# Output copies of the last heads at high priority, low halves of later weights behind the last 1/std of a layer, and another order of V, of the last norm and of the first logits

## The chip, the cores and the metric

One core of one Trainium2 chip runs the whole kernel as one program. The metric is the time on the device in microseconds (us). The kernel before takes 1009.29 us, the median of three runs (1008.67 to 1011.96).

A core has five engines, each with its own queue of instructions, which it works off in the order in which they were put there: TensorE (PE in the profile; PEld is its loading of weights), VectorE (DVE), ScalarE (ACT), GpSimd (POOL) and SyncE (SP), which here issues the DMAs. An instruction that needs another engine's result waits for a semaphore, and all that stands behind it on its engine waits with it.

## The reference

A decoder trunk of four layers over 512 tokens of width 1024, in float32. Layer i uses mixer i mod 3, so the layers (counted from 0) are latent attention (MLA), sliding-window attention (SWA), forgetting attention (FoX), MLA. Each branch has one input projection that also gives a gate; after each stands a LayerNorm over the residual:

```python
def reference(x, ln_g, ln_b, ...):
    for i in range(DEPTH):                     # DEPTH = 4
        ...
        x = _layernorm(DEEPNORM_ALPHA * x + y, ln_g[i], ln_b[i])

def _fox_branch(x, w_in, b_f, w_out):
    h = x @ w_in
    q, k, v = ...                              # 16 heads of 64
    f_logit = h[..., 3 * W:3 * W + FOX_HEADS]
    cum = jnp.cumsum(jax.nn.log_sigmoid(f_logit + b_f), axis=1)
    o = _dense_causal(q, k, v, FOX_HEAD_DIM ** -0.5, cum)
    return (o * jax.nn.silu(gate)) @ w_out
```

MLA projects x to 672 columns (384 for the query, 256 for key and value, 32 for the rotary key), norms them, and projects these up to heads; its causal attention is like FoX's without the gates.

## The kernel before, in words

**Arithmetic.** Every float32 operand is split in a high half, rounded to the type that TensorE takes (fp32r), and a low half, the rest. A product is three matmuls: high by high, high by low, low by high. For weights the high half is a cast on ScalarE (L306) and the low half a subtraction on GpSimd (L310), from a raw tile `wr` that SyncE loaded; for activations ScalarE casts the high half and VectorE subtracts (L325). A *unit* is one piece of weights of up to 1024 columns. `W(key)` (called where a projection begins) sees to it that the unit and up to three behind it are split; `hold` is the last unit that it may go ahead to; `_split(i)` splits all units up to i. A unit has an even and an odd tile in the tables below: `w` high, the next `w` low.

**A layer.** The normed x of 512 tokens is kept transposed, `xT` (high and low), in four token blocks of 128. First come projections from `xT`: for MLA the compressed columns in two groups T0 and T1 of 336 columns for each token block (`t_block`, order `T_ORDER`), 24 matmuls each, whose results VectorE copies to `cqk` and ScalarE squares for `t_norm`; for FoX the first V groups, V0 (256 columns and the 16 gate logits, 272) and V1 (256), 24 matmuls for each token block (`vproj`). Three PSUM banks (`pp`) take such results. Then 16 heads run interleaved with the remaining projections: logits (`ss`), softmax, transposes of the probabilities (`ptt`) and the product with V (`oo`), whose two halves are added by a copy on ScalarE and an addition on VectorE (L543, L544) into `o`; there is one bank for `oo`. The output projection (`po`, `pp`) ends the layer.

**What sets the order.** During the heads TensorE's order is written out by hand: the strings in `ORDER`, one for each layer, take steps of the logits (s), the transposes (t), the products with V (o) and the other projections (f, g, h); `TAIL` does it for the last two heads. In `finish` the string `FINISH[layer]` sets VectorE's order: for token block t, `r t` (or `h t`, `i t` for its halves) adds the output projection to the residual in tile `r` with its sum, `s t` starts the sum of squares on ScalarE, `t t` computes 1/std, whose power runs on GpSimd (L646, `stat<-stat,half`), `a t` scales by mean and gain, `b t` by 1/std with the bias (both L660, two instructions of 512 columns), and `x t` transposes the block into the next layer's `xT` (`pxt` L389, eight transposes, a cast on ScalarE, the low half on VectorE). All that no string sets (ScalarE, GpSimd, SyncE, and TensorE outside the heads) is ordered when the kernel is built, by a scheduler with costs of its own; `high_priority` makes it prefer what stands inside. Of the last layer the last block is normed in halves (`p`, `q`), the scaled result goes into tile `y`.

**The start.** Blocks of x are loaded and transposed; `mla(0)` begins with T0 and T1 while raw weights still arrive.

Of the kernel before, what the change touches and what calls it, by code (L numbers as in the profile page):

```python
# [16 lines left out]
ALU = mybir.AluOpType  # L17
# [12 lines left out]
QR, KR = 384, 256  # L30
# [13 lines left out]
)  # L44
PRO = ((2, 1, 2, 2), (2, 1, 19, 0))
TAIL = ((3, 4, 6, 6), (2, 10, 2, 5), (9, 0, 4, 9), (6, 3, 7, 2))


VF_COLS, VF_K = 256 + H, (3, 3, 2)
T_COLS = 336  # L50
T_ORDER = (((0, 0), (0, 1), (1, 0), (1, 1), (0, 2), (1, 2), (0, 3), (1, 3)),
           ((0, 0), (1, 0), (0, 1), (1, 1), (0, 2), (1, 2), (0, 3), (1, 3)))

def jobs(s):
# [12 lines left out]
ORDER = (  # L67
# [133 lines left out]
class Net:  # L201
# [178 lines left out]
    def x_transposes(self, xt, tb, banks=None):  # L380

        nc = self.nc
        for g in range(2):
            pool, tag = banks or (self.ps_t, "pt")
            ps = pool.tile([128, 512], F32, tag=tag, name=self.nm("pxt"))
            for k in range(4):
                c = (4 * g + k) * 128
                v = ps[:, k * 128:(k + 1) * 128]
                nc.tensor.transpose(v, xt[:, c:c + 128], self.ident[:])  # L389
# [3 lines left out]
            nc.scalar.copy(hi, src)  # L393
            self.lo(lo, src, hi)
# [130 lines left out]
    def attn_pv(self, h, st):  # L525
        nc = self.nc
# [11 lines left out]
        p, odd = divmod(h, 2)  # L538
# [3 lines left out]
        a, b = (slice(64, 128), slice(0, 64)) if odd else (slice(0, 64), slice(64, 128))  # L542
        nc.scalar.copy(o[a, :], o_ps[b, :])  # L543
        nc.vector.tensor_tensor(o[a, :], o_ps[a, :], o[a, :], op=ALU.add)  # L544
        if odd:
# [82 lines left out]
    def ln_other_half(self, st, tb):  # L628

        nc = self.nc  # L630
        e, s = st["half"], st["stat"][:, tb]
        nc.vector.tensor_scalar(s[:, 2:3], s[:, 0:1], s[:, 1:2], -1.0 / D, op0=ALU.add, op1=ALU.mult)
        jk = self.p_g.tile([128, D // 2], BF16, tag="g", name=self.nm("jk"))
        nc.scalar.activation(jk[:], st["r"][tb][:, D // 2:], AF.Square, bias=s[:, 2:3], scale=1.0, accum_out=e[:, 2:3])
        nc.vector.tensor_tensor(e[:, 3:4], s[:, 2:3], e[:, 0:1], op=ALU.subtract)
        nc.vector.tensor_scalar(e[:, 3:4], e[:, 3:4], e[:, 3:4], D / 2.0, op0=ALU.mult, op1=ALU.mult)
        nc.vector.tensor_tensor(e[:, 3:4], e[:, 3:4], e[:, 1:2], op=ALU.add)

    def ln_rstd(self, st, tb):
# [5 lines left out]
        nc.vector.tensor_scalar(s, s, 1.0 / D, LN_EPS, op0=ALU.mult, op1=ALU.add)
        nc.gpsimd.tensor_tensor(s, s, self.half[:, 0:1], op=ALU.pow)  # L646

    def ln_apply(self, layer, st, tb, part):
        nc = self.nc
# [3 lines left out]
        src = r  # L653
        if halves and part == 0:

            r = st["r"][tb] = self.p_wr.tile([128, D], F32, tag="wr", name=self.nm("y"))
        for c in range(2):
            cols = slice(c * 512, (c + 1) * 512)
# [60 lines left out]
    def finish(self, layer, st):  # L719
        nc = self.nc  # L720
        self.load_gb(layer, st)
        self.layer = layer + 1
        if layer < DEPTH - 1:
            self.new_xT()
# [13 lines left out]
        def ends(tb):  # L738
            assert st["done"] >= (84, 105, 126, 147)[tb]
            mm(0, tb)  # L740
            if tb < 3:
# [4 lines left out]
                "r": lambda t: (res(t, 0), res(t, 1)), "h": lambda t: res(t, 0), "i": lambda t: res(t, 1), "s": S0, "t": S1,  # L746
                "a": lambda t: A(t, 0), "b": lambda t: A(t, 1), "p": lambda t: self.ln_half(st, t), "q": lambda t: self.ln_other_half(st, t), "x": X}
        if "p3" in FINISH[layer]:
            st["halves"] = NT - 1
            st["half"] = self.p_st.tile([128, 4], F32, tag="half", name=self.nm("half"))  # L750
        with self.tc.manual_schedule(engines={mybir.EngineType.DVE}):
            for w in FINISH[layer].split():
                todo[w[0]](int(w[1:]))

    def cq_done(self, layer):
# [12 lines left out]
    def mla(self, layer):  # L768
# [19 lines left out]
        def t_norm(tb):  # L788
# [5 lines left out]
            with self.tc.high_priority():  # L794
                nc.gpsimd.tensor_tensor(rr[:, tb, :], rr[:, tb, :], self.half[:, :2], op=ALU.pow)
            nc.vector.tensor_scalar(x[:, :QR], x[:, :QR], rr[:, tb, 0:1], None, op0=ALU.mult)
            nc.vector.tensor_scalar(x[:, QR:QR + KR], x[:, QR:QR + KR], rr[:, tb, 1:2], None, op0=ALU.mult)
            kr, c, d = x[:, 640:672], x[:, 672:704], x[:, 704:736]
# [6 lines left out]
        self.hold = self.index[(layer, "T", 1, 3)]  # L805
        for t, tb in T_ORDER[layer > 0]:
            if (t, tb) == (1, NT - 1):
                self.hold = len(self.units)
            t_block(t, tb)
            if t == 1:  # L810
                t_norm(tb)
# [94 lines left out]
        vs = {}  # L906
# [135 lines left out]
    def fox(self, layer):  # L1042
# [9 lines left out]

        for tb in range(NT):
            self.run(self.vproj([(layer, "V", 0, b) for b in range(3)], 8, self.xblk, vs, 0, [tb], f_logit))
            self.run(vp(1, [tb]))
        nc.scalar.activation(e[:], z[:], AF.Abs)
# [52 lines left out]
def trunk(ctx, tc, t):  # L1109
# [13 lines left out]
    for tb in range(NT):  # L1123
        net.x_transposes(x0[tb], tb)
    for layer in range(DEPTH):
        (net.mla, net.swa, net.fox)[layer % 3](layer)
# [31 lines left out]
```

## Time and profile before

| | |
|---|---|
| profiled execution | 1012.59 us |
| its span | 1010.8 us |
| granted TensorE clock, mean | 0.993 |
| median of three runs | 1009.29 us |
| busy: TensorE, ScalarE, VectorE, GpSimd | 981.7, 620.0, 599.2, 505.4 us |

The busy time of an engine is the time in which it executes something; the idle times of TensorE and what ended them are in the views that the prediction quotes. A row of a timeline has its start, its length, the engine, the line of the kernel, the operation, and output and inputs by name; consecutive instructions of one group make one row with their number, and the brackets hold the idle time before it and what it waited for.

### The profile page before, as it was taken

What the parts mean: (1) busy time and instruction counts of PE and PEld (TensorE: products, weight loads), DVE (VectorE), ACT (ScalarE), POOL (GpSimd) and SP (SyncE); (2) the same over time, 40 slices, a digit from 0 to 9 for tenths busy, and PEclk for the clock granted to TensorE, in tenths of its full rate; (3) what the DMA queues carried; (4) which work ended last, traced back from release to release, by engine and by line L of the source; (5) the groups of instructions that cost most, each with busy time, mean ns of one, the idle gap of its engine ahead of it and who ended that gap; (6) DMA issues with size and microseconds to landing.
All of it is one profiled execution on the core that took longest, in us unless ns stands there. A gap on an engine that the chain in (4) does not pass through costs nothing.

```text
span 1010.8 us, 16221 instructions
## 1 busy us (share of the span) xinstructions
PE 981.7 (97%) x5512; PEld 854.6 (85%) x5512; DVE 599.2 (59%) x1509; ACT 620.0 (61%) x1355; POOL 505.4 (50%) x568
## 2 busy tenths in 40 slices
PE   8999999999999999999999999999999999999996
PEld 8978888878888888888988898888779888888785
DVE  2467676944736667729324655567456476668827
ACT  4378888753256777723446766666443588888722
POOL 5846656334146663433455757553263746664211
PEclk9999999999999999999999999999999999999999
DMA  6453332543542222334344334326233354324322
GB/s 224 124 151 87 112 87 85 165 154 98 188 125 84 75 73 101 112 99 150 102 140 125 105 85 146 104 82 186 88 117 114 108 137 129 94 87 123 107 63 84
DMA packets 37795, 116.79 MB, mean 116 GB/s; under 512 B 5440, under 2 KB 5696, under 8 KB 37456
## 3 DMA queue, kind: packets, MB, share of 16 engines
q1 hardware_dynamic: 37712, 115.75, 36.9%
q8 instruction: 44, 0.72, 0.3%
q14 instruction: 39, 0.32, 0.1%
HBM read 92.62 MB, written 8.42 MB: 100 GB/s over the span
## 4 chain that ended last, share of the span: by engine, by line
PE 45%; DVE 3%; issue 3%; POOL 2%; ACT 1%; DMA 1%; DVEq 0%; POOLq 0%; SPq 0%; ACTq 0%
PE pp L322 30%; PE ss L322 4%; PE po L322 4%; PE oo L322 3%; PE ptt L514 3%; POOL w L310 1%; DVE r L660 1%; PE pxt L389 1%; DMA cb<-cd 0%; DVE PT L325 0%; DMA q<-rq 0%; ACT PT L500 0%; DVE r L590 0%; DVE wo L310 0%; PE pc L823 0%
## 5 line engine op out<-in xcount | busy, mean ns | idle before, releaser
L322 PE MATMUL pp<-xT,w 128*128 128x512 f32 (+1 forms) x1440 | 352.5, 387 | 0.0
L310 POOL TENSOR_TENSOR w<-wr,w 128x512 fp32r<-128x512 f32 (+1 forms) x202 | 241.9, 1223 | 193.4 <-ACT w L306 128.2
L322 PEld LDWEIGHTS pp<-xT,w 128*128 128x128 f32 x1440 | 256.1, 188 | 44.2
L462 POOL TENSOR_TENSOR P<-P,rs 128x256 f32<-128x256 f32 (+2 forms) x192 | 113.2, 618 | 128.4 <-DVE rs L457 123.1
L306 ACT CAST w<-wr 128x1024 fp32r<-128x1024 f32 (+5 forms) x121 | 116.1, 964 | 87.7 <-PE pp L322 44.2
L451 ACT ACTIVATE P<-P,m 128x256 f32<-128x256 f32 (+3 forms) x256 | 137.7, 539 | 45.1 <-DVE m L1086 17.3
L325 DVE TENSOR_TENSOR PT<-ptt,PT 128x384 fp32r<-128x384 f32 (+1 forms) x176 | 104.1, 600 | 48.7 <-ACT PT L500 47.3
L322 PE MATMUL pp<-w,xT 128*128 128x256 f32 (+2 forms) x768 | 112.9, 300 | 2.3 <-ACT xT L393 1.8
L322 PE MATMUL oo<-PT,v 128*128 128x256 f32 (+3 forms) x512 | 106.6, 313 | 5.3 <-DVE o L544 4.6
L500 ACT CAST PT<-ptt 128x384 fp32r<-128x384 f32 (+1 forms) x176 | 88.4, 515 | 35.6 <-PE ptt L514 24.7
L322 PEld LDWEIGHTS pp<-w,xT 128*128 128x128 f32 x768 | 106.1, 191 | 4.0 <-ACT xT L393 2.5
L322 PEld LDWEIGHTS oo<-PT,v 128*128 128x128 f32 x512 | 83.3, 189 | 17.2 <-DVE o L544 6.0
L322 PE MATMUL ss<-kt,q 128*128 128x128 f32 (+3 forms) x384 | 81.7, 328 | 2.2 <-ACT kt L855 1.6
L322 PE MATMUL pp<-cT,w 128*128 128x512 f32 x312 | 81.6, 397 | 0.0
L514 PE MATMUL ptt<-ident,P 128*128 128x128 f32 x480 | 78.6, 275 | 2.0 <-POOL P L462 1.1
L902 DVE CUSTOM_DVE_ANT_0 P<-ss,mask 128x128 f32<-128x128 f32 (+3 forms) x128 | 61.1, 485 | 32.3 <-PE ss L322 24.5
L322 PE MATMUL pp<-w,oT 128*128 128x512 f32 x288 | 76.1, 398 | 0.0
L322 PE MATMUL po<-wo,oT 128*128 128x512 f32 x288 | 71.6, 396 | 0.0
L322 PEld LDWEIGHTS ss<-kt,q 128*128 128x128 f32 x384 | 60.7, 189 | 8.8 <-ACT kt L855 2.2
L514 PEld LDWEIGHTS ptt<-ident,P 128*128 128x128 f32 x480 | 57.1, 140 | 12.5 <-POOL P L462 2.1
L544 DVE TENSOR_TENSOR o<-oo,o 64x512 f32<-64x512 f32 x64 | 43.9, 686 | 37.5 <-ACT o L543 36.7
L322 PEld LDWEIGHTS pp<-cT,w 128*128 128x128 f32 x312 | 56.6, 188 | 10.4
(126 smaller groups left out, 1420.8 us busy)
## 6 DMA issues: line engine op xcount, KB each, us to landing
wr<-in_w SPq DMA_DIRECT2D x106, 512.0 KB, 3.5
q<-rq SPq DMA_DIRECT2D x64, 128.0 KB, 2.3
xd<-r SPq DMA_DIRECT2D x12, 512.0 KB, 2.9
r<-xd SPq DMA_DIRECT2D x12, 512.0 KB, 3.5
wr<-in_w SPq DMA_DIRECT2D x16, 336.0 KB, 3.4
kd<-kd SPq DMA_DIRECT2D x20, 256.0 KB, 3.3
tq<-in_cs SPq DMA_DIRECT2D x8, 512.0 KB, 3.9
cb<-cd SPq DMA_DIRECT2D x16, 256.0 KB, 3.9
```

The costliest lines, as they stand in the source:

```text
L306: nc.scalar.copy(w[0][:, :c], r[:, :c])
L310: eng.tensor_tensor(w[1][:, a:b], r[:, a:b], w[0][:, a:b].bitcast(F32), op=ALU.subtract)
L322: self.nc.tensor.matmul(out, l, r, start=start, stop=stop)
L325: (eng or self.nc.vector).tensor_tensor(out, src, hi.bitcast(F32), op=ALU.subtract)
L389: nc.tensor.transpose(v, xt[:, c:c + 128], self.ident[:])
L451: nc.scalar.activation(v, v, AF.Exp, bias=m[:, c:c + 1], scale=-1.0, accum_out=sums[:, c:c + 1])
L462: nc.gpsimd.tensor_tensor(v, v, rs[:, c:c + 1].to_broadcast([128, v.shape[1]]), op=ALU.mult)
L500: nc.scalar.copy(pt[:, 0, :n], ps[:, :n])
L514: nc.tensor.transpose(ps[:, c:c + 128], Ps[qb][:, kb * 128:(kb + 1) * 128], self.ident[:])
L544: nc.vector.tensor_tensor(o[a, :], o_ps[a, :], o[a, :], op=ALU.add)
L660: nc.vector.scalar_tensor_tensor(r[:, cols], in0=src[:, cols], scalar=s[:, k:k + 1], in1=st["gb"][2 * part + c][:], op0=op, op1=(ALU.mult, ...
L902: nc.vector.tensor_tensor_reduce(out=P[:, :n], in0=ps[:, :n], in1=self.mask[:, S - n:], scale=1.0, scalar=3e38, op0=ALU.add, op1=ALU.min, ...
```

## The change

- `attn_pv`: the copy and addition that empty the bank of `oo` stand at high priority for heads 13, 14 and 15.
- `finish`: `hold` is set to a unit of the next layer (`EARLY`) while `FINISH` runs, and behind it the units up to `LATE` are split with `issue_after`, a wait in the order of building: they stand behind the last 1/std of the layer (`st["pow"]`).
- `fox`: V0 of all four token blocks, then V1 of all four, where V0 and V1 alternated.
- `T_ORDER`: layer 3 takes the order that layer 0 had. `t_norm`: two scalings at high priority.
- the last layer: the residual and the sum of squares of block 2 stand ahead of the first scaling; the scaling of the last block by mean and gain is in two parts (`c`, `d`), between which the rest of 1/std stands (`e`, `t`).
- `ORDER` and `TAIL`: first logits of layers 0, 1 and 3, and the end of layer 2.
- the start: the first split of a weight stands behind the first cast of x.

```diff
+EARLY, LATE = (2, 3, 4, 0), (5, 5, 8, 0)
-TAIL = (..., (9, 0, 4, 9), ...)
+TAIL = (..., (7, 6, 4, 5), ...)
-T_ORDER = (((0, 0), (0, 1), (1, 0), (1, 1), (0, 2), (1, 2), (0, 3), (1, 3)),
-           ((0, 0), (1, 0), (0, 1), (1, 1), (0, 2), (1, 2), (0, 3), (1, 3)))
+T_ORDER = ((0, 0), (0, 1), (1, 0), (1, 1), (0, 2), (1, 2), (0, 3), (1, 3))
 FINISH, last layer
-    '... s0 s1 a0 t0 r2 s2 t1 a1 b0 t2 b1 h3 p3 a2 b2 i3 q3 a3 t3 b3',
+    '... s0 s1 r2 s2 a0 t0 t1 a1 b0 t2 b1 h3 p3 a2 b2 i3 q3 c3 e3 t3 d3 b3',
 ORDER, first steps of layers 0, 1 and 3
-    "s9 f6 s6 f6 s3 f6 s3 f9 t1 ...
+    "f6 s6 f3 s3 f3 s6 f6 s3 f3 s3 f6 t1 ...
-    "f2 s4 f10 s10 f19 s2 f1 s2 t7 ...
+    "f2 s2 f4 s2 f4 s2 f4 s2 f4 s2 f4 s2 f6 s2 f3 s2 f1 s2 t7 ...
-    "f6 s2 f6 s4 f6 s3 g6 ...
+    "f12 s3 f3 s3 f3 s3 g6 ...
 x_transposes
-            nc.scalar.copy(hi, src)
+            self.cast = nc.scalar.copy(hi, src).ins
 attn_pv
-        nc.scalar.copy(o[a, :], o_ps[b, :])
-        nc.vector.tensor_tensor(o[a, :], o_ps[a, :], o[a, :], op=ALU.add)
+        with self.tc.high_priority() if h >= H - 3 else nullcontext():
+            nc.scalar.copy(o[a, :], o_ps[b, :])
+            nc.vector.tensor_tensor(o[a, :], o_ps[a, :], o[a, :], op=ALU.add)
 ln_rstd
-        nc.gpsimd.tensor_tensor(s, s, self.half[:, 0:1], op=ALU.pow)
+        st["pow"] = nc.gpsimd.tensor_tensor(s, s, self.half[:, 0:1], op=ALU.pow).ins
 finish
+        first = self.index[(layer, "O", 1, 3)] + 1
+        self.hold = first + EARLY[layer] - 1
...
             for w in FINISH[layer].split():
                 todo[w[0]](int(w[1:]))
+        self.hold = len(self.units)
+        if layer < DEPTH - 1:
+            with self.tc.issue_after(st["pow"]):
+                self._split(first + LATE[layer] - 1)
 fox
-        for tb in range(NT):
-            self.run(self.vproj([(layer, "V", 0, b) for b in range(3)], 8, self.xblk, vs, 0, [tb], f_logit))
-            self.run(vp(1, [tb]))
+        self.run(self.vproj([(layer, "V", 0, b) for b in range(3)], 8, self.xblk, vs, 0, range(NT), f_logit))
+        self.run(vp(1))
 trunk
         net.x_transposes(x0[tb], tb)
+        if tb == 0:
+            with tc.issue_after(net.cast):
+                net._split(0)
```

How this moves instructions is seen in the order in which each engine has them. GpSimd, at the boundary of layers 2 and 3, before (`stat` is the 1/std of a block, `w` and `wo` the low halves of layer 3's first weights, two instructions for each):

```order
L310 TENSOR_TENSOR w_1537_8001<-wr_1532_7982,w_1536_8000 128x160
L310 TENSOR_TENSOR w_1563_8199<-wr_1538_8005,w_1562_8198 128x512
L310 TENSOR_TENSOR w_1563_8199<-wr_1538_8005,w_1562_8198 128x160
L646 TENSOR_TENSOR stat_1083_5728<-stat_1083_5728,half_121 128x1
L310 TENSOR_TENSOR w_1566_8206<-wr_1561_8196,w_1565_8205 128x512
L310 TENSOR_TENSOR w_1566_8206<-wr_1561_8196,w_1565_8205 128x160
L310 TENSOR_TENSOR w_1560_8192<-wr_1535_7992,w_1559_8191 128x512
L310 TENSOR_TENSOR w_1560_8192<-wr_1535_7992,w_1559_8191 128x160
L646 TENSOR_TENSOR stat_1083_5728<-stat_1083_5728,half_121 128x1
L310 TENSOR_TENSOR wo_1568_8212<-wr_1564_8203,wo_1568_8212 128x512
```

and after the change, at the same place:

```order
L312 TENSOR_TENSOR w_1537_8001<-wr_1532_7982,w_1536_8000 128x512
L312 TENSOR_TENSOR w_1537_8001<-wr_1532_7982,w_1536_8000 128x160
L654 TENSOR_TENSOR stat_1083_5728<-stat_1083_5728,half_121 128x1 x4
L312 TENSOR_TENSOR w_1553_8183<-wr_1535_7992,w_1552_8182 128x512
L312 TENSOR_TENSOR w_1553_8183<-wr_1535_7992,w_1552_8182 128x160
L312 TENSOR_TENSOR w_1556_8190<-wr_1538_8005,w_1555_8189 128x512
L312 TENSOR_TENSOR w_1556_8190<-wr_1538_8005,w_1555_8189 128x160
L312 TENSOR_TENSOR w_1559_8197<-wr_1554_8187,w_1558_8196 128x512
```

The four 1/std stand together, and five low halves that stood ahead of or between them stand behind the fourth; `w_1553` is the low half that belongs to the last quarter of T0. At the other two boundaries it is the same with three (1 to 2) and four (0 to 1) units.

TensorE at the same boundary, after the change, behind 20 matmuls for T0 of the second token block (`pp_1575`); `pp_1573` is T0 of the first, `pp_1577` T1 of the first, `pxt_1548` and `pxt_1549` the transposes of the third block:

```order
L324 MATMUL pp_1575_8253<-w_1552_8182,xT_1528_7973 128x336 x2
L324 MATMUL pp_1577_8281<-w_1555_8189,xT_1528_7973 128x336 x2
L391 MATMUL pxt_1548_8153<-ident_116,r_1447_7568 128x128 x4
L391 MATMUL pxt_1549_8160<-ident_116,r_1447_7568 128x128 x4
L324 MATMUL pp_1573_8225<-w_1553_8183,xT_1528_7973 128x336
L324 MATMUL pp_1573_8225<-w_1552_8182,xT_1528_7973 128x336 x2
```

The matmuls with `w_1553` have moved behind those of both blocks with the rest of T0; before, each block's T0 was finished with 24 matmuls in one piece and T1 of the same block came next. TensorE at the boundary of layers 1 and 2, after the change (`pp_1032` and `pp_1033` are V0 of the first and second token block, `pxt_1014` to `pxt_1017` the transposes of the second and third):

```order
L324 MATMUL pp_1032_5253<-w_1004_5025,xT_995_5000 128x272
L391 MATMUL pxt_1014_5178<-ident_116,r_933_4694 128x128 x4
L391 MATMUL pxt_1015_5185<-ident_116,r_933_4694 128x128 x4
L324 MATMUL pp_1033_5281<-w_997_5004,xT_995_5000 128x272
L391 MATMUL pxt_1016_5199<-ident_116,r_934_4696 128x128 x4
L391 MATMUL pxt_1017_5206<-ident_116,r_934_4696 128x128 x4
L324 MATMUL pp_1033_5281<-w_997_5004,xT_995_5000 128x272
```

Before, 24 matmuls of V1 (`128x256`) for the first token block stood around `pxt_1014`, `pxt_1015` and ahead of `pxt_1016`; they have moved behind V0 of the later blocks.

More of the change, by code (lines that the diff above doesn't have):

```diff
@@ L1 @@
 import math
-from contextlib import ExitStack
+from contextlib import ExitStack, nullcontext
 from itertools import chain, islice
@@ L42 @@
     'f33 k3 f99 k0 k1 r0 s0 r1 t0 m4 a0 k2 s1 b0 t1 a1 x0 b1 m4 r2 h3 s2 a2 x1 t2 i3 b2 s3 t3 a3 b3 x2 x3',
[1 row of a table removed]
[1 row of a table added]
 )
+EARLY, LATE = (2, 3, 4, 0), (5, 5, 8, 0)
 PRO = ((2, 1, 2, 2), (2, 1, 19, 0))
-TAIL = ((3, 4, 6, 6), (2, 10, 2, 5), (9, 0, 4, 9), (6, 3, 7, 2))
+TAIL = ((3, 4, 6, 6), (2, 10, 2, 5), (7, 6, 4, 5), (6, 3, 7, 2))
 VF_COLS, VF_K = 256 + H, (3, 3, 2)
 T_COLS = 336
-T_ORDER = (((0, 0), (0, 1), (1, 0), (1, 1), (0, 2), (1, 2), (0, 3), (1, 3)),
-           ((0, 0), (1, 0), (0, 1), (1, 1), (0, 2), (1, 2), (0, 3), (1, 3)))
+T_ORDER = ((0, 0), (0, 1), (1, 0), (1, 1), (0, 2), (1, 2), (0, 3), (1, 3))
 def jobs(s):
@@ L634, in ln_other_half, with ln_move @@
         nc.scalar.activation(jk[:], st["r"][tb][:, D // 2:], AF.Square, bias=s[:, 2:3], scale=1.0, accum_out=e[:, 2:3])
+    def ln_move(self, st, tb):
+        nc = self.nc
+        e, s = st["half"], st["stat"][:, tb]
         nc.vector.tensor_tensor(e[:, 3:4], s[:, 2:3], e[:, 0:1], op=ALU.subtract)
@@ L645, in ln_rstd, with ln_apply @@
         nc.vector.tensor_scalar(s, s, 1.0 / D, LN_EPS, op0=ALU.mult, op1=ALU.add)
-        nc.gpsimd.tensor_tensor(s, s, self.half[:, 0:1], op=ALU.pow)
-    def ln_apply(self, layer, st, tb, part):
+        st["pow"] = nc.gpsimd.tensor_tensor(s, s, self.half[:, 0:1], op=ALU.pow).ins
+    def ln_apply(self, layer, st, tb, part, cs=(0, 1)):
         nc = self.nc
@@ L653, in ln_apply @@
         src = r
+        if halves and part == 0 and cs[0] == 0:
+            r = st["r"][tb] = self.p_wr.tile([128, D], F32, tag="wr", name=self.nm("y"))
         if halves and part == 0:
-            r = st["r"][tb] = self.p_wr.tile([128, D], F32, tag="wr", name=self.nm("y"))
-        for c in range(2):
+            src = st["whole"] = st.get("whole", src)
+        for c in cs:
             cols = slice(c * 512, (c + 1) * 512)
@@ L746, in finish @@
                 "r": lambda t: (res(t, 0), res(t, 1)), "h": lambda t: res(t, 0), "i": lambda t: res(t, 1), "s": S0, "t": S1,
-                "a": lambda t: A(t, 0), "b": lambda t: A(t, 1), "p": lambda t: self.ln_half(st, t), "q": lambda t: self.ln_other_half(st, t), "x": X}
+                "a": lambda t: A(t, 0), "b": lambda t: A(t, 1), "p": lambda t: self.ln_half(st, t), "q": lambda t: self.ln_other_half(st, t), "x": X,
+                "c": lambda t: self.ln_apply(layer, st, t, 0, (0,)), "d": lambda t: self.ln_apply(layer, st, t, 0, (1,)),
+                "e": lambda t: self.ln_move(st, t)}
         if "p3" in FINISH[layer]:
@@ L795, in t_norm @@
                 nc.gpsimd.tensor_tensor(rr[:, tb, :], rr[:, tb, :], self.half[:, :2], op=ALU.pow)
-            nc.vector.tensor_scalar(x[:, :QR], x[:, :QR], rr[:, tb, 0:1], None, op0=ALU.mult)
-            nc.vector.tensor_scalar(x[:, QR:QR + KR], x[:, QR:QR + KR], rr[:, tb, 1:2], None, op0=ALU.mult)
+            with self.tc.high_priority():
+                nc.vector.tensor_scalar(x[:, :QR], x[:, :QR], rr[:, tb, 0:1], None, op0=ALU.mult)
+                nc.vector.tensor_scalar(x[:, QR:QR + KR], x[:, QR:QR + KR], rr[:, tb, 1:2], None, op0=ALU.mult)
             kr, c, d = x[:, 640:672], x[:, 672:704], x[:, 704:736]
@@ L805, in mla @@
         self.hold = self.index[(layer, "T", 1, 3)]
-        for t, tb in T_ORDER[layer > 0]:
+        for t, tb in T_ORDER:
             if (t, tb) == (1, NT - 1):
```

8 rows, old and new, of tables (FINISH, ORDER) are left out of this document.

## The prediction

> **What bounds the kernel now.** I read the page's first part, then TensorE's waits.
>
> ```profile
> span 1010.8 us, 16221 instructions
> PE 981.7 (97%) x5512; PEld 854.6 (85%) x5512; DVE 599.2 (59%) x1509; ACT 620.0 (61%) x1355; POOL 505.4 (50%) x568
> ```
>
> TensorE is busy 981.7 of 1010.8 us and no other engine comes near, so the number of matmuls, which the change leaves alone, fixes nearly everything. All that an order can win is the other 29.1 us and whatever half clock there is. The waits of TensorE, summed by what ended them (us in total, times, longest), say where it is:
>
> ```profile
> PE oo L322 <- DVE o L544: 4.6, 4, 1.5
> PE pxt L389 <- DVE r L660: 4.5, 4, 2.2
> ```
>
> The first four waits are for a head's output copy before the next head may use the one bank; the second four are transposes of the normed x that wait for VectorE at the boundary of two layers. The timeline of TensorE (start, us, work, idle before it in brackets) places the latter:
>
> ```profile
> 253.25 0.66 PE L389 MATMUL pxt<-ident,r 128*128 128x128 f32 x4 [0.24 <-DVE r L660]
> 254.93 0.66 PE L389 MATMUL pxt<-ident,r 128*128 128x128 f32 x4 [1.02 <-DVE r L660]
> 462.41 0.66 PE L389 MATMUL pxt<-ident,r 128*128 128x128 f32 x4 [1.02 <-DVE r L660]
> 752.48 0.66 PE L389 MATMUL pxt<-ident,r 128*128 128x128 f32 x4 [2.18 <-DVE r L660]
> 753.40 0.66 PE L389 MATMUL pxt<-ident,r 128*128 128x128 f32 x4 [0.27 <-DVE stat L645]
> ```
>
> Why VectorE is late there is in its own timeline and GpSimd's:
>
> ```profile
> 251.41 3.46 DVE L660 SCALAR_TENSOR_TENSOR r<-r,stat,ln_b 128x512 f32<-128x512 f32 x2
> 458.75 3.06 POOL L310 TENSOR_TENSOR w<-wr,w 128x512 fp32r<-128x512 f32 x2
> 458.89 3.46 DVE L660 SCALAR_TENSOR_TENSOR r<-r,stat,ln_b 128x512 f32<-128x512 f32 x2
> 471.66 1.42 DVE L660 SCALAR_TENSOR_TENSOR r<-r,stat,ln_b 128x512 f32<-128x512 f32 x2 [0.23 <-POOL stat L646]
> ```
>
> The pair of scalings (L660, called b below) takes 1.42 us with GpSimd idle and 3.46 while GpSimd makes low halves of the next weights. Last comes the granted clock, from windows of time: length, busy time (count) of PE, PEld, DVE, ACT, POOL, then clock, DMA share, GB/s.
>
> ```profile
> 252.40:255.80 3.40, 2.14 (x13) 1.43 (x12) 3.08 (x3) 0.76 (x2) 1.93 (x2) 1.00 0.77 233
> 255.80:259.20 3.40, 3.40 (x24) 3.05 (x23) 2.74 (x7) 0.41 (x1) 1.52 (x2) 1.00 1.03 401
> 419.60:423.00 3.40, 1.69 (x12) 1.40 (x12) 2.02 (x4) 1.88 (x5) 1.54 (x3) 1.00 0.00 0
> 423.00:426.40 3.40, 3.40 (x16) 3.29 (x15) 2.92 (x11) 1.55 (x4) 1.53 (x2) 0.50 0.00 0
> 750.60:754.00 3.40, 1.25 (x9) 1.02 (x10) 3.33 (x4) 2.27 (x4) 3.40 (x4) 1.00 0.45 113
> 754.00:757.40 3.40, 3.40 (x10) 2.68 (x9) 3.40 (x5) 1.34 (x2) 3.40 (x4) 0.51 0.93 292
> ```
>
> After 1.71 and 2.15 us of idle in 3.4 the next 3.4 us ran at half clock, which costs 1.7 us each; after 1.26 they did not. A stall of over some 1.5 us is thus paid twice.
>
> **The change, part by part.** Sums are against the profiled execution (1012.59 us, 3.3 above the median of 1009.29; about two half-clock windows); negative is faster.
>
> *Output copies at high priority*: no copy of o, on ScalarE or VectorE, stands in another place of its engine's order in any layer. 0, and the 4.6 us of waits stay.
>
> *Boundary of layers 0 and 1*: the four 1/std now run together and the low halves behind them, so b takes 1.42. That removes 0.24 + 1.02; weight halves w behind the last 1/std arrive about when TensorE asks. **−1.2**; bounds −1.7 to +0.5, if a late half costs as much as the wait that goes.
>
> *Boundary of layers 1 and 2, and the order of V*.
>
> ```profile
> 462.82 3.72 PE L322 MATMUL pp<-wo,oT 128*128 128x512 f32 x15
> 466.38 3.76 PE L322 MATMUL pp<-w,xT 128*128 128x272 f32 x29
> 472.99 1.28 DVE L325 TENSOR_TENSOR xT<-pxt,xT 128x512 fp32r<-128x512 f32 x2
> 474.42 0.99 POOL L646 TENSOR_TENSOR stat<-stat,half 128x1 f32<-128x1 f32 x1 [2.79 <-PE pxt L389]
> 475.91 1.41 DVE L660 SCALAR_TENSOR_TENSOR r<-r,stat,ln_b 128x512 f32<-128x512 f32 x2
> ```
>
> The first b (458.89) ends 2.0 earlier and all of VectorE behind it too. The second transposes start near 461.1 instead of 462.41: −1.3. The 15 matmuls (3.5) and V's 24 of token block 0 (3.76 by 29 is 0.13 at most; 3.0) then end at 468.0. Before, 24 matmuls of V's second group followed; they filled the time until block 1 was normed. Now TensorE goes to the transposes of blocks 1 and 2 at once. The latter need b of block 2, 471.66 − 2.0 = 469.65 and half a pair more: 470.4, where TensorE stands from 469.1. Wait 1.3; and block 1's low half (472.99 − 2.0 + 0.65) costs 0.1. Block 1's V ends at 474.5. The last 1/std ends at about 473.4, and there GpSimd begins the weights that were held, just as the last b begins (475.91 − 2.0 = 473.9): by the rows of 458 it takes 3.46, its halves end at 475.7 and 477.4, and the two transposes wait 1.2 and 1.3. Sum +2.6. Of V's second group 72 matmuls stood ahead of the last log-gate and now stand behind it; the chain from the gates to the first softmax ends that much earlier, which should remove a wait there:
>
> ```profile
> 551.15 0.33 PE L514 MATMUL ptt<-ident,P 128*128 128x128 f32 x1 [0.42 <-POOL P L462]
> ```
>
> −0.4, so **+2.2**; bounds −1.7 (no wait takes the old one's place) to +4.3 (2.5 us of idle within 3 earn a half-clock window).
>
> *Boundary of layers 2 and 3*.
>
> ```profile
> 750.67 2.68 DVE L660 SCALAR_TENSOR_TENSOR r<-r,stat,ln_b 128x512 f32<-128x512 f32 x2 [0.32 <-POOL stat L646]
> 753.82 4.59 PE L322 MATMUL pp<-wo,oT 128*128 128x512 f32 x12
> 757.09 2.03 DVE L660 SCALAR_TENSOR_TENSOR r<-r,stat,ln_b 128x512 f32<-128x512 f32 x2
> 758.24 5.66 PE L322 MATMUL pp<-w,xT 128*128 128x336 f32 x36
> ```
>
> Removed: 2.18 + 0.27 idle, and 1.7 of half clock behind it (the 12 matmuls take 4.59 instead of 2.8): −4.1. Then, with VectorE's pairs at 1.41: b of block 0 at 750.0, so its transposes still wait 0.65; the 12 matmuls end at 754.6, T's 20 (0.157 each, 5.66 by 36) at 757.7. Next now stands block 1 of the same T, where before 16 matmuls of the other T stood: its squares and cast end near 759.3, its low half at 760.0: wait 1.4. Its 20 end at 763.0, and four transposes later (764.2) TensorE needs w behind the last 1/std (about 764.0 by the chain of residual, square, 1/std): 1.25 to 1.5 us for GpSimd's half, so 1.3 of wait, and all three banks are held, so nothing else can run. The last b is slowed again: 0.85 for the last transposes; 0.4 for the next halves. Adds 4.6: **+0.5**; bounds −3.5 (only the first 0.65 stays) to +2.2 (half clock).
>
> *Starts of layers*.
>
> ```profile
> 62.03 0.33 PE L322 MATMUL ss<-kt,q 128*128 128x128 f32 x1 [0.79 <-ACT kt L855]
> 63.93 0.69 DVE L325 TENSOR_TENSOR kt<-pp,kt 64x512 fp32r<-64x512 f32 x1
> 298.73 1.30 PE L322 MATMUL ss<-kd,q 128*128 128x128 f32 x6 [0.38 <-DVE m L964]
> 811.46 0.33 PE L322 MATMUL ss<-kt,q 128*128 128x128 f32 x1 [0.80 <-ACT kt L855]
> ```
>
> Layer 0: the logits that filled in between now stand behind V, whose second block waits for the bank that VectorE frees at 64.4 (63.93 + 0.69, a little earlier): 2.0 of wait where 1.0 was, **+0.9** (0 to +1.5). Layer 1: the burst of ten logits is spread: **−0.4** (−1.0 to 0). Layer 3: V takes the place of one wait and meets the next, **−0.1** (−0.8 to +0.8).
>
> *Prologue*.
>
> ```profile
> 7.71 0.42 PE L322 MATMUL pp<-w,xT 128*128 128x336 f32 x1 [1.82 <-ACT xT L393]
> ```
>
> The cast of x goes ahead of that of the first weight, so this starts up to 0.5 sooner, but behind two matmuls stand transposes of a block of x that is not loaded yet: **0** (−0.5 to +0.5).
>
> *Last norm*, from the timeline of all engines:
>
> ```profile
> 997.61 3.85 PE L322 MATMUL pp<-wo,oT 128*128 128x512 f32 x16
> 1001.02 1.41 DVE L660 SCALAR_TENSOR_TENSOR r<-r,stat,ln_b 128x512 f32<-128x512 f32 x2
> 1002.34 0.68 DVE L590 SCALAR_TENSOR_TENSOR r<-r,pp 128x512 f32<-128x512 f32 x1
> 1003.91 1.41 DVE L660 SCALAR_TENSOR_TENSOR y<-r,stat,P 128x512 f32<-128x512 f32 x2
> 1005.65 0.55 POOL L646 TENSOR_TENSOR stat<-stat,half 128x1 f32<-128x1 f32 x1 [6.92 <-DVE stat L645]
> ```
>
> The last residual begins when b of block 2 lets it, 0.88 behind the last matmul (997.61 + 3.85); with two residuals moved ahead of that chain it begins at once, −0.8. The 1/std moves between the halves of the first scaling and runs beside the second half: 0.74 off the chain, 0.45 back if it takes 0.99 beside VectorE, as at 474.42: −0.4. **−1.2** (−1.6 to −0.8).
>
> Sum: −1.2 + 2.2 + 0.5 + 0.9 − 0.4 − 0.1 + 0 − 1.2 = **+0.7**: 1013.3 for an execution like the profiled one, 1010.0 on the median.
>
> One rule speaks against the terms for half clock. The Trainium skill, TensorE: Matmul & The Clock Gate, Part 1, has the clock fall after at least one idle window of about 3.4 us, free-running; by it no wait forecast here would slow TensorE, the upper bounds would fall by 1.7 each and the second rival would stand at 1010.6. The trace differs (half clock after 1.71 us of idle in 3.4), and I go by the trace.
>
> **The rivals.** *The new waits do not come* (0.31): the last b runs at 1.42 beside GpSimd, and the held halves are there before TensorE is (764.2). For it: the pairs of 750 and 757 (2.68, 2.03) lie between the two prices, and in three boundaries GpSimd has time enough. Against it: both rows of 3.46, and that GpSimd's held work begins with the very instruction that lets b go. Without them only −1.2, −1.7, −3.5, +0.9, −0.4, −0.1 and −1.2 are left: −7.2, or 1002. It decides from the point at which b's slow-down is under half.
>
> *The held weights set the end* (0.27, slower): GpSimd stands idle until the last 1/std and then everything waits for it at both later boundaries; the idle of 2.5 us near 477 and of 2.2 near 766 falls into one window of 3.4 each, so half clock follows twice: +0.7 + 3.4 and 0.5 for slower low halves, 1014. It decides from about 1.5 us of idle in a window.
>
> *The copies do not move* is no longer a rival: the order shows it, and the forecast has it. Had they moved, at most 4.6 was to be won.
>
> **How the numbers follow.** The forecast as summed has 0.42. A difference under 0.3% (3 us) is about what a measurement can tell from none: 1006.3 to 1012.3. Faster is the first rival, 0.31; same the forecast, 0.42; slower the second, 0.27. The range, 1003 to 1014.5, leaves out the ends of both.
>
> **What would show it.** Right: waits of oo for the copies still near 4.6; first b of each boundary at 1.4; the transposes of V's block 2 and the last block in layer 2 waiting over 1 us each, the last b near 3.4; matmuls that wait for GpSimd's w behind the last 1/std at 764; the end 8.2 us behind the last matmul where it was 9.35. Wrong: no wait for w at the last boundary, or an idle of under 1 us there; a layer 0 start without its second wait; half clock in places that no stall explains.

## The result and the profile after

| | before | the change |
|---|---|---|
| median of the first comparison | 1009.54 us (4 runs, 1008.67 to 1011.96) | 1017.85 us (4 runs, 1017.19 to 1021.44) |
| ratio | | 1.0086, 95% interval 1.0056 to 1.0115 |
| again, with more runs on one chip | 1012.91 us (29 runs) | 1018.69 us (6 runs) |
| ratio | | 1.0059, interval 1.0040 to 1.0079 |
| profiled execution | 1012.59 us | 1017.29 us |

One of the 29 runs of before took 1206.56 us at a mean clock of 0.75, and the ratio leaves it out.

The kernel became slower, by about 6 us; the forecast was 0.7 more, and both measurements lie above its range. The 4.7 us between the two profiled executions can be laid out by place, since TensorE has the same 5512 matmuls in both and is busy for the same time (981.6 us after, 981.7 before). The table takes the start of TensorE's n-th matmul in an execution, less the start of the n-th in the first profile of before, and shows by how much this lag grows in each stretch, in us. Its last two columns are further profiled executions, from the experiments below: the change again (1020.21 us) and the kernel before again (1011.73 us).

| stretch (us in the first profile of before) | forecast | the change | the change again | before again |
|---|---|---|---|---|
| prologue and start of layer 0 (to 91) | +0.9 | +1.3 | +3.3 | +0.1 |
| boundary of layers 0 and 1 (249 to 272) | −1.2 | −1.2 | −1.2 | 0.0 |
| start of layer 1 (272 to 358) | −0.4 | +0.5 | +0.7 | 0.0 |
| boundary of layers 1 and 2 (454 to 543) | +2.6 | +2.6 | +2.6 | 0.0 |
| the wait at 551 (543 to 594) | −0.4 | −0.6 | −0.3 | −0.7 |
| boundary of layers 2 and 3, start of layer 3 (742 to 833) | +0.4 | +3.1 | +4.0 | +0.2 |
| behind the last matmul | −1.2 | −0.9 | −0.9 | 0.0 |
| all the rest | 0 | −0.1 | −0.5 | −0.5 |
| the whole span | +0.7 | +4.7 | +7.6 | −0.9 |

First the waits of TensorE after the change, summed by what ended them (us in total, times, longest):

```profile
PE oo L324 <- DVE o L547: 4.6, 4, 1.6
PE pp L324 <- POOL w L312: 2.5, 1, 2.5
PE pp L324 <- DVE q L904: 2.1, 2, 1.1
PE pxt L391 <- DMA x<-in_x: 1.7, 1, 1.7
PE pxt L391 <- DVE r L670: 1.7, 2, 1.1
```

The copies' waits are the same 4.6. The transposes' waits for VectorE fell from 4.5 to 1.7. New are waits for GpSimd's low halves, for VectorE in the start of layer 0, and for a load of x. The timeline of TensorE after the change places them (start, us, work, idle before it and what ended it):

```profile
9.51 1.92 PE L391 MATMUL pxt<-ident,x 128*128 128x128 f32 x8 [1.72 <-DMA x<-in_x]
62.88 0.94 PE L324 MATMUL pp<-w,cT 128*128 128x256 f32 x6 [1.10 <-DVE q L904]
65.11 0.95 PE L324 MATMUL pp<-w,cT 128*128 128x256 f32 x6 [1.29 <-DVE kt L327]
254.18 1.04 PE L391 MATMUL pxt<-ident,r 128*128 128x128 f32 x8
304.79 0.33 PE L1006 MATMUL ptt<-ident,P 128*128 128x128 f32 x1 [0.59 <-POOL P L464]
471.00 1.33 PE L391 MATMUL pxt<-ident,r 128*128 128x128 f32 x8 [0.72 <-issue]
477.66 0.63 PE L391 MATMUL pxt<-ident,r 128*128 128x128 f32 x4 [1.09 <-DVE r L670]
753.46 1.32 PE L391 MATMUL pxt<-ident,r 128*128 128x128 f32 x8 [0.57 <-DVE r L670]
763.38 3.49 PE L324 MATMUL pp<-w,xT 128*128 128x336 f32 x21 [1.16 <-DVE xT L327]
770.21 1.65 PE L324 MATMUL pp<-w,xT 128*128 128x336 f32 x6 [2.46 <-POOL w L312]
```

The boundary of layers 0 and 1 runs through without a gap (254.18 has none). The other two have lost their old wait and got others, the longest at 770. What the clock made of that one, in the windows around it (length, busy time of PE, PEld, DVE, ACT, POOL, then clock, DMA share, GB/s):

```profile
767.50:770.90 3.40, 0.94 (x7) 0.70 (x6) 3.34 (x5) 0.98 (x3) 3.11 (x3) 0.97 0.39 121
770.90:774.30 3.40, 3.40 (x16) 3.29 (x15) 2.86 (x5) 0.00 (x0) 3.40 (x4) 0.53 0.64 198
```

So behind 2.46 us of idle TensorE ran a window at half clock, and the work in it took 1.7 us longer. Whether that made the whole longer is seen below, in the second profile of the change, which has the same wait without it. And the engines that made it wait: VectorE's scalings and GpSimd's work at the last two boundaries, after the change:

```profile
459.43 1.41 DVE L670 SCALAR_TENSOR_TENSOR r<-r,stat,ln_b 128x512 f32<-128x512 f32 x2
473.86 7.29 POOL L312 TENSOR_TENSOR w<-wr,w 128x512 fp32r<-128x512 f32 x5
474.06 3.46 DVE L670 SCALAR_TENSOR_TENSOR r<-r,stat,ln_b 128x512 f32<-128x512 f32 x2
752.66 1.41 DVE L670 SCALAR_TENSOR_TENSOR r<-r,stat,ln_b 128x512 f32<-128x512 f32 x2
761.31 1.42 DVE L670 SCALAR_TENSOR_TENSOR r<-r,stat,P 128x512 f32<-128x512 f32 x2 [1.31 <-ACT jk L621]
765.98 0.20 DVE L619 TENSOR_SCALAR stat<-stat 128x1 f32<-128x1 f32 x1
767.56 0.15 DVE L653 TENSOR_SCALAR stat<-stat 128x1 f32<-128x1 f32 x1 [1.37 <-ACT jk L621]
767.79 0.98 POOL L654 TENSOR_TENSOR stat<-stat,half 128x1 f32<-128x1 f32 x1 [3.18 <-PE pxt L391]
768.75 6.24 POOL L312 TENSOR_TENSOR w<-wr,w 128x512 fp32r<-128x512 f32 x6
```

The first b of each boundary takes 1.41 us instead of 3.46 and 2.68, as meant. The last b of layer 1 takes the 3.46 instead: the slow-down has moved from the first block to the last one. In layer 2 the last b takes 2.69, the last 1/std ends at 768.77, and w comes behind it.

### The profile page after: what moved, and what is told of

It reads as the page before. It is cut to its first block, busy times and chain, and to the rows that moved or that the text cites. A ratio compares the mean times of both kernels' runs of the same rounds, so it can differ in the third digit from the quotient of the medians.

```text
span 1015.5 us, 16224 instructions
## 1 busy us (share of the span) xinstructions
PE 981.6 (97%) x5512; PEld 853.7 (84%) x5512; DVE 594.0 (58%) x1509; ACT 619.5 (61%) x1355; POOL 504.3 (50%) x568
## 4 chain that ended last, share of the span: by engine, by line
PE 44%; DVE 5%; issue 2%; ACT 2%; DMA 1%; POOL 1%; POOLq 0%; DVEq 0%; SPq 0%; ACTq 0%
PE pp L324 29%; PE ss L324 4%; PE oo L324 4%; PE po L324 3%; PE ptt L516 3%; DVE r L670 2%; DVE r L593 1%; DMA wr<-in_w 1%; DMA q<-rq 0%; POOL w L312 0%; DVE xT L327 0%; ACT jk L621 0%; DVE PT L327 0%; ACT PT L502 0%; POOL stat L654 0%
## 5 line engine op out<-in xcount | busy, mean ns | idle before, releaser
L654 POOL TENSOR_TENSOR stat<-stat,half 128x1 f32<-128x1 f32 x16 | 13.7, 858 | 100.3 <-DVE stat L653 97.2
```

What stands on the lines that cost most here:

```text
L654: st["pow"] = nc.gpsimd.tensor_tensor(s, s, self.half[:, 0:1], op=ALU.pow).ins
```

## The experiments

Every ratio is to the kernel before, run beside it on the same chip. The first set had 27 runs of before (median 1011.65 us), the second 29 (1012.91), the third 23 (1012.62).

**Is the base sound?** The kernel before, again, no edit.

> The kernel before, profiled once more. Theory A: the execution that was profiled first held two windows of half clock in its middle (423 and 754 us) that a usual run does not hold, so a run near 1009 us shows at most one of them; of the 8.3 us between the medians about 3.4 are then no work of the change but the profile that was taken as the base. Rival B: a run near 1009 us shows both windows and is shorter somewhere else; the change itself then costs all 8.3 in stalls.

1011.18 us (10 runs), ratio 0.999 (0.9968 to 1.0012). Its profiled execution, 1011.73 us, has the window of half clock at the third boundary too:

```profile
749.60:753.00 3.40, 0.75 (x5) 0.52 (x6) 3.08 (x6) 2.25 (x4) 3.40 (x4) 1.00 0.30 101
753.00:756.40 3.40, 3.40 (x11) 2.77 (x12) 3.40 (x4) 1.41 (x3) 3.40 (x4) 0.55 1.01 275
```

and one at 422, as the first profile. So both profiled executions of before have both windows, and Theory A falls for them; a run near 1009 us was not profiled. But its other half holds: 10 and 27 runs of one program spread from 1008.7 to 1016.5 us, and the four of the first comparison lay at the short end. The profiled execution of before, 1012.59, was a usual one. One thing differs in the second profile: TensorE has no wait at 551 us, where the first had 0.42.

**The wait for w at the last boundary.** T0's last quarter is split without being held; the rest of the change is kept.

```diff
+        if layer == 2:
+            self._split(first + 3)
         if layer < DEPTH - 1:
             with self.tc.issue_after(st["pow"]):
```

> The change, but the last quarter of T0's weights of layer 3 is split as early as before; the other held units stay behind the last 1/std. Theory A: the wait of 2.5 us for GpSimd's low half at 770 and the half clock behind it (1.7) are a net cost: about 4 us less than the change, 1013.5 to 1014. Rival B: TensorE meets the next late thing there (the last block's second scaling, beside GpSimd, or the next held unit): under 1.5 us less, 1016.5 or more.

1015.9 us, ratio 1.0031 (1.0013 to 1.0049); profiled 1013.71, where the change had 1017.29. TensorE at that place:

```profile
754.07 0.66 PE L391 MATMUL pxt<-ident,r 128*128 128x128 f32 x4 [1.02 <-DVE stat L653]
769.18 0.42 PE L324 MATMUL pp<-w,xT 128*128 128x336 f32 x1 [0.53 <-ACT xT L395]
770.58 1.19 PE L324 MATMUL pp<-w,xT 128*128 128x336 f32 x6 [0.98 <-POOL w L312]
```

The wait of 2.46 is gone, but a wait of 0.98 for the next held unit, T1's first, and one of 1.02 at the first b have come, as rival B has it. 2.8 us by the ratios (1.0059, the change measured again below, less 1.0031; each has about 0.002 to either side) lie between A's 4 and B's 1.5.

**The slow last b.** At the boundary of layers 1 and 2 GpSimd's held units wait for the last b.

```diff
+            after = st["pow"]
+            if layer == 1:
+                dm = self.p_st.tile([128, 1], F32, tag="dm", name=self.nm("dm"))
+                after = nc.gpsimd.tensor_tensor(dm[:], st["r"][3][:, D - 1:], self.half[:, 0:1], op=ALU.mult).ins
-            with self.tc.issue_after(st["pow"]):
+            with self.tc.issue_after(after):
```

> The change, but at the boundary of layers 1 and 2 GpSimd's held units wait for the last second scaling (b) of VectorE instead of the last 1/std; one tiny multiplication on GpSimd reads its result. Theory A: b takes 1.4 us instead of 3.46, the waits of 0.46 and 1.09 at 476 and 478 go, 1.5 us less than the change (1016.3). Rival B: the units are then late for V1 or for the keys behind it, and the time stays (1017.5 to 1018.5).

1016.18 us, ratio 1.0031 (1.0016 to 1.0045), profiled 1015.76. VectorE's last two scalings of layer 1, and TensorE and GpSimd beside them:

```profile
474.95 1.41 DVE L670 SCALAR_TENSOR_TENSOR r<-r,stat,ln_b 128x512 f32<-128x512 f32 x2
476.22 1.04 PE L391 MATMUL pxt<-ident,r 128*128 128x128 f32 x8
476.58 2.55 POOL L312 TENSOR_TENSOR w<-wr,w 128x512 fp32r<-128x512 f32 x2
```

The last b takes 1.41 instead of 3.46 with GpSimd's first low half behind it, the transposes run as one row without a gap, and V1 waits for nothing: Theory A for the mechanism. The ratio fell by 0.0028, twice the 1.5 us forecast, with an uncertainty as large as that. By the profile, the lag grows by 0.5 us between 454 and 543 where it grew by 2.6 in the change.

**No holding at all.**

```diff
-        self.hold = first + EARLY[layer] - 1
-            with self.tc.issue_after(st["pow"]):
-                self._split(first + LATE[layer] - 1)
```

> The change without its holding of weights (no EARLY, no LATE, no wait for the last 1/std) at all three boundaries; V order, order of T0 and T1 and all else kept. Theory A: the holding is a loss at the last two boundaries and a gain at the first: the wait of 2.5 with its half clock goes (4.2), the slow last b in layer 1 goes (1.5), the slow first b of each boundary comes back (1.3, 1.3 and 1.6): 1.5 less in all, about 1016. Rival B: with the order of V and T of the change the fillers are missing either way, and all waits of before come back on top: 1018 or more. Rival C: the holding is all of the loss: 1010 or less.

1019.54 us, ratio 1.0064 (1.0042 to 1.0085): no better than the change. TensorE's waits at the last two boundaries:

```profile
466.68 0.66 PE L391 MATMUL pxt<-ident,r 128*128 128x128 f32 x4 [1.02 <-DVE r L670]
475.69 0.39 PE L324 MATMUL pp<-w,xT 128*128 128x272 f32 x1 [1.00 <-ACT xT L395]
476.79 1.79 PE L391 MATMUL pxt<-ident,r 128*128 128x128 f32 x8 [0.71 <-issue]
760.07 0.65 PE L391 MATMUL pxt<-ident,r 128*128 128x128 f32 x4 [2.21 <-DVE r L670]
```

Rival B: the slow first b is back (1.02 and 2.21), and the two waits of V's new order (1.00 and 0.71) are there without any holding. So the order of V costs by itself; C, the holding as all of the loss, falls. The last boundary is different. Behind its 2.21 and another 0.28 stands only one wait, of 0.24 at 770, and the lag grows by 0.7 us there, not by the 3.1 and 4.0 of the two profiles of the change. So T's order, which this run keeps, costs little there by this profile, and the holding is what costs.

**Each later boundary undone as a whole.** First V's order and the holding in layer 1:

```diff
-        self.hold = first + EARLY[layer] - 1
+        if layer != 1:
+            self.hold = first + EARLY[layer] - 1
...
-        if layer < DEPTH - 1:
+        if layer in (0, 2):
             with self.tc.issue_after(st["pow"]):
...
-        self.run(self.vproj([(layer, "V", 0, b) for b in range(3)], 8, self.xblk, vs, 0, range(NT), f_logit))
-        self.run(vp(1))
+        for tb in range(NT):
+            self.run(self.vproj([(layer, "V", 0, b) for b in range(3)], 8, self.xblk, vs, 0, [tb], f_logit))
+            self.run(vp(1, [tb]))
```

> The change without its order of V in layer 2 and without holding weights at the boundary of layers 1 and 2; all else kept. Theory A: this place alone holds +2.6 us (460 to 480) less the wait of 0.7 at 551 that comes back: about 2 us less than the change. Rival B: the two parts pay for each other later in layer 2, and the time does not move.

1014.33 us, ratio 1.0028 (1.0012 to 1.0044): 3.1 us less than the change (0.0031 of 1010), near A's 2. Then T's order and the holding in layer 2, with V's kept:

```diff
-T_ORDER = ((0, 0), (0, 1), ...
+T_ORDER = (((0, 0), (0, 1), ...), ((0, 0), (1, 0), ...))
...
-        self.hold = first + EARLY[layer] - 1
+        if layer != 2:
+            self.hold = first + EARLY[layer] - 1
...
-        if layer < DEPTH - 1:
+        if layer < 2:
             with self.tc.issue_after(st["pow"]):
...
-        for t, tb in T_ORDER:
+        for t, tb in T_ORDER[layer > 0]:
```

> The change without its order of T0 and T1 in layer 3 and without holding weights at the boundary of layers 2 and 3; all else kept. Theory A: this place holds +3.3 us (750 to 780), half of it half clock: 3 us less than the change, and the long wait of TensorE there is again for VectorE's first scaling beside GpSimd. Rival B: nothing or under 1 us, since the first scaling's wait of 2.2 and its half clock come back in full.

1013.4 us, ratio 1.0010 (0.9992 to 1.0028): 4.9 us less than the change (2.6 to either side), so this one place holds the largest part of the loss. Its TensorE there has the old wait again, and behind it no other:

```profile
755.85 0.66 PE L392 MATMUL pxt<-ident,r 128*128 128x128 f32 x4 [2.09 <-DVE r L671]
756.78 0.66 PE L392 MATMUL pxt<-ident,r 128*128 128x128 f32 x4 [0.28 <-DVE stat L654]
757.19 3.02 PE L325 MATMUL pp<-wo,oT 128*128 128x512 f32 x12
```

The 12 matmuls behind 2.4 us of idle took 3.02, at full clock; in the first profile of before the same 12 took 4.59 behind the same idle. Half clock after such a wait is frequent, not certain; the last section shows on what it depends.

**The change again, and what is worth keeping**, on the same chip.

> The change itself once more, in more rounds beside the kernel before. Theory A: the first comparison stood on four runs of before that fell at the short end (27 runs in the first set had 1008.9 to 1016.5, median 1011.65); the change is about 5 us slower, as its stalls in the two profiles add up (4.8), a ratio near 1.005. Rival B: the four runs were typical; the ratio stays at 1.008 or above.

Ratio 1.0059 (1.0040 to 1.0079): A. The profiled execution of this set has the wait for w without half clock behind it:

```profile
772.54 1.19 PE L324 MATMUL pp<-w,xT 128*128 128x336 f32 x6 [2.48 <-POOL w L312]
775.16 1.21 PE L324 MATMUL pp<-w,xT 128*128 128x336 f32 x6 [0.25 <-POOL w L312]
776.88 0.91 PE L324 MATMUL pp<-w,xT 128*128 128x336 f32 x4 [0.50 <-POOL w L312]
778.35 0.58 PE L324 MATMUL pp<-wo,xT 128*128 128x336 f32 x2 [0.57 <-ACT wo L308]
```

At full clock TensorE waits again, for GpSimd's next held halves, for ScalarE's cast of `wo`, and once more for 0.35 at 779. The stretch from 742 to 833 costs 4.0 us here, 3.2 in the run with the spared last b, also without half clock at this place, and 3.1 with it in the first profile. So the half clock is not what made the stretch long: it passed in time in which TensorE would else have waited for the held units.

The kernel that keeps only the first boundary's holding, the last norm, the priorities and TAIL has, beside the orders of V and T of the two before, also

```diff
-        self.hold = first + EARLY[layer] - 1
+        if layer == 0:
+            self.hold = first + EARLY[layer] - 1
...
-        if layer < DEPTH - 1:
+        if layer == 0:
             with self.tc.issue_after(st["pow"]):
...
-        if tb == 0:
-            with tc.issue_after(net.cast):
-                net._split(0)
```

and the ORDER of before.

> Of the change only the holding of weights at the boundary of layers 0 and 1, the order of the last norm, the high priorities and the end of layer 2 (TAIL); starts of layers, V, T and the later boundaries as before. Theory A: 1.3 us less at 254 and 0.9 less behind the last matmul: 2 us faster than before, a ratio near 0.998, and no other place moves. Rival B: a wait that is saved early comes back at the next wait for the same engine (at 208 and 421 us a head's copy), so it is 1 us or less.

1010.5 us, ratio 0.9975 (0.9962 to 0.9988): faster than before, by 2.5 us where A says 2. At the first boundary its TensorE has no gap, and the last 1/std and the last scaling stand at the end:

```profile
253.12 1.03 PE L392 MATMUL pxt<-ident,r 128*128 128x128 f32 x8
1002.06 0.99 POOL L655 TENSOR_TENSOR stat<-stat,half 128x1 f32<-128x1 f32 x1 [6.90 <-DVE stat L654]
1003.08 1.42 DVE L671 SCALAR_TENSOR_TENSOR y<-y,stat,ln_b 128x512 f32<-128x512 f32 x2 [0.44 <-POOL stat L655]
```

**The starts alone**, put into the kernel before: ORDER of the change (with it the first steps of layers 0, 1 and 3), and

```diff
+        if tb == 0:
+            with tc.issue_after(net.cast):
+                net._split(0)
```

> The kernel before with only the change's starts: the first steps of ORDER of layers 0, 1 and 3 and its prologue (TAIL of layer 2 as in the change). Theory A: the start of layer 0 costs more than forecast, since its two waits (1.1 and 1.3) fall into one window of the clock and earn a half-clock window (1.7); prologue +0.6, layer 0 +1.0 to 2.4, layer 1 +0.7: 2.3 to 3.7 us slower, a ratio of 1.002 to 1.004. Rival B: as forecast, +0.5 us, a ratio within 0.001 of 1.

1014.31 us, ratio 1.0019 (1.0006 to 1.0031): slower, nearer to A than to the forecast. (Its TAIL is that of before; the text on record says otherwise.) The windows at the start of layer 0:

```profile
62.00:65.40 3.40, 1.15 (x7) 0.77 (x6) 3.18 (x5) 2.88 (x6) 2.38 (x2) 1.00 0.94 278
65.40:68.80 3.40, 3.27 (x12) 2.91 (x13) 0.85 (x2) 0.56 (x2) 0.07 (x1) 0.57 0.70 189
```

2.25 us of idle in 3.4, and half clock behind. Of the eight profiled executions with this start six have half clock here and take 2.3 to 3.7 us more than before up to 91 us; the first profile of the change and the run with T0's last quarter early have the same two waits without it and take 1.3 more.

**Better placed holding?** To the kernel that keeps the first boundary and the last norm: at the later boundaries the held units start behind the first b.

```diff
+                if w == "b0" and layer in (1, 2):
+                    dm = self.p_st.tile([128, 1], F32, tag="dm", name=self.nm("dm"))
+                    st["dm"] = nc.gpsimd.tensor_tensor(dm[:], st["r"][0][:, D - 1:], self.half[:, 0:1], op=ALU.mult).ins
...
-        if layer == 0:
-            with self.tc.issue_after(st["pow"]):
+        if layer < DEPTH - 1:
+            with self.tc.issue_after(st["pow"] if layer == 0 else st["dm"]):
+                self._split(first + LATE[layer] - 1)
```

> The last kernel of the second set (first boundary and last norm), and at the boundaries of layers 1 and 2 and of 2 and 3 GpSimd's low halves of the next weights start behind the first block's second scaling (a tiny multiplication on GpSimd reads its result) and run between the 1/std of the later blocks; orders of V and T as before. Theory A: what delays TensorE there is the first b beside GpSimd, and nothing needs the halves before the later blocks: 1.2 us less at 460 and 2 to 4 less at 750 than in that kernel, a ratio to before near 0.994. Rival B: the later scalings are slowed in its place and the halves come late: no faster than that kernel, 0.9975 or more.

1015.78 us, ratio 1.0027 (1.0012 to 1.0042): rival B, and worse. The 1/std of the second block now stands behind GpSimd's units, and the second b beside them:

```profile
754.59 6.16 POOL L313 TENSOR_TENSOR w<-wr,w 128x512 fp32r<-128x512 f32 x6
760.71 0.55 POOL L655 TENSOR_TENSOR stat<-stat,half 128x1 f32<-128x1 f32 x1
761.29 2.67 DVE L671 SCALAR_TENSOR_TENSOR r<-r,stat,ln_b 128x512 f32<-128x512 f32 x2 [3.22 <-POOL stat L655]
```

TensorE waits 3.1 us there, at 764. But by the profile most of the loss is at the boundary of layers 1 and 2, where the lag grows by 4.2 us (0.4 at the later one). There too the 1/std of the second block stands behind GpSimd's units and its b, beside them, takes 3.48; TensorE then waits in two places, and two windows of half clock follow (473 to 480):

```profile
473.05 0.72 PE L325 MATMUL pp<-w,xT 128*128 128x272 f32 x2 [1.64 <-ACT xT L396]
474.38 1.97 PE L392 MATMUL pxt<-ident,r 128*128 128x128 f32 x8 [0.61 <-DVE r L671]
```

At these two boundaries, in each of the placements that ran beside the norm, some block's b was slowed.

## Why the prediction was wrong

The step that failed is the boundary of layers 2 and 3. By the ratios the change costs 5.9 per mille, some 6 us; in per mille, undoing its parts gives 3.1 (V and the boundary of layers 1 and 2) and 4.9 (T and the boundary of layers 2 and 3), the starts cost 1.9 alone, and what is left gains 2.5. These sum to 7.4, which the intervals (0.0012 to 0.002 each way) allow.

- *Copies at high priority: 0.* Right; 4.6 us of waits before and after.
- *Boundary of layers 0 and 1, and last norm: −1.2 and −1.2.* Right as mechanisms: the slow first b and the gaps at 253 and 255 went, −1.2 in both profiles. The kernel that kept the two gained 2.5. The last norm's own share is less than forecast, 8.5 us behind the last matmul instead of 9.35, so −0.9; its 1/std took 0.99 beside VectorE, which the forecast had reckoned with.
- *Boundary of layers 1 and 2: +2.2.* Right step by step up to 543 us: 0.54, 0.72, 0.46 and 1.09 us of waits in the places named, the last b at 3.46, and 2.6 in sum, as forecast, in both profiles. Undoing it gave 3.1. The −0.4 for the wait at 551 is not borne out: that wait is missing in the second profile of before too, and in the runs with V's old order (V undone, the kept parts, the starts alone), and the change again has 0.17 of it. That it was gone in the first profile of the change was luck; that V's order shortens the chain from the gates is not shown.
- *Boundary of layers 2 and 3: +0.5.* **This step failed.** Undoing it gave 4.9, and the two profiles have 3.1 and 4.0 there. TensorE's first waits came as forecast (0.57 for 0.65; 0.33 and 1.16 for 1.4). The wait for w was 2.46 instead of 1.3, because the last 1/std was put at "about 764.0 by the chain of residual, square, 1/std", 9.4 us behind the start of T; it ended 11.4 us behind it (768.77 less 757.39), while TensorE came only 0.8 later. The prediction does not show how it reckoned the chain, but the rows of after have two links that its three words leave out. The scaling of the third block by mean and gain works in place in r, and so waits for ScalarE's square that still reads r (761.31, 1.31 of idle). And the mean of the last block, without which its square cannot start, stands behind the b of the block before it in VectorE's order (765.98); 1/std then waits 1.37 for the square. The string of `FINISH` has this order ("b2 s3 t3"), which the change leaves alone, and so have the rows of before:

```profile
767.29 1.41 DVE L660 SCALAR_TENSOR_TENSOR r<-r,stat,ln_b 128x512 f32<-128x512 f32 x2
768.61 0.21 DVE L616 TENSOR_SCALAR stat<-stat 128x1 f32<-128x1 f32 x1
```

The second term of this step that was too small is the 0.4 for the next halves. GpSimd works off what was held in one row of 6.24 us, and TensorE, which needs it piece by piece, waits another 0.25 and 0.50 for it in the second profile, and 0.57 and 0.35 for ScalarE; in the first the half clock passed in this time. The 0.85 for the last transposes did not come at all. Freeing T0's last unit alone took 2.8 us off by the ratios.

- *Starts: +0.4 in sum.* Too small; 1.9 alone. Layer 0's two waits were forecast as 2.0 and are 2.4; that half clock may follow them was not reckoned with, though the prediction had just read from the windows that it follows such idle, and it did in six of eight executions. The prologue's two gaps sum to 3.05 us, where before's were 2.1: a transpose ahead of its load waits 1.72 for the DMA, "0" in the forecast (2.6 in the second profile of the change). Layer 1 was forecast as −0.4 and is +0.5 to +0.7: the wait moved from the logits to the transposes (0.59 and 0.24 at 305).
- *The base.* The sum was carried to a median of three runs as if the profiled execution were 3.3 long by bad luck. It was not; the medians of before in the three sets are 1011.65 to 1012.91. Carried so, the forecast would have been 1012.4 to 1013.6, and the change is 1018 to 1019.

Of the rivals the slower one named the cause, the held weights that set the end at the later boundary, but took its loss for half clock behind 477 and 766. It did not follow at 477 in the profiled runs of the change, and where it followed, at 770, it did not lengthen the stretch. The faster one, that the new waits do not come, was wrong: nearly all came.

What stays open: how much of each ratio is half clock, since one or two profiles for a kernel do not give its frequency; and why the last boundary costs 3.1, 4.0, 3.2 and, in the run with V undone, 1.8 us in the four profiled executions that share its order and its holding. In the last of these the wait for w is 0.92, behind half clock at 762, and the later ones are 0.25 in all.

## What to carry to other kernels

Holding back one engine's work to spare another's moves the slow-down to whatever runs when the work is let go; it pays only where nothing waits for either, as at the first boundary here. When replaying an order, follow reads that an in-place write must wait for, and the rank of each small instruction in its queue, since the last link of a norm's chain sets when held work begins. And a work order that brings two transposes together takes away the matmuls that hid their norm.

## What the runs showed that was not expected

The time of one program spreads by 8 us (1008.85 to 1016.51 in 27 runs on one chip), and the four runs of the first comparison had a median 2 to 3 us below those of the three sets; on which chip they ran is not on record.

Part of the spread that the profiles show is half clock. It comes in stretches of 3.41 us, at times two in a row, and within one profile the stretches begin whole multiples of 3.41 us apart. Laid on this grid, in all twelve profiles behind their first 20 us, every one of the 13 windows at full clock with 1.80 us of idle or more (up to 2.46) was followed by half clock, 10 of the 20 with 1.50 to 1.79, and one with less. So the prediction's "over some 1.5 us" has about the right size, but it holds for the idle within one window of the grid. A wait that falls across a border is divided: in the second profile of the change the idle around its 2.48 us lies 1.71 and 1.03 in two windows, and both were followed by full clock.

```profile
768.35:771.76 3.41, 1.70 (x14) 1.45 (x12) 2.04 (x6) 2.20 (x4) 1.64 (x2) 1.00 0.57 194
771.76:775.17 3.41, 2.38 (x17) 2.12 (x17) 3.41 (x5) 0.00 (x0) 3.41 (x4) 1.00 0.24 47
```

The wait of 2.37 us in the run with T's order undone is divided in the same way (1.73 in the fuller window). The power for one 1/std on GpSimd, 128 numbers, took 0.55 us alone and 0.98 to 1.11 beside VectorE's scalings.
